# Splitting the row-bound step of the activations' scale, and reordering the parts and squares of the last blocks

## Chip, cores and metric

The program runs on one core of a Trainium2 chip. The metric is the device time of one execution in microseconds. All rows below come from one profiled execution.

## What is computed

One layer of a hybrid encoder, in float32, for 512 tokens of 1024 channels. The two attention-like branches come first; the change touches only the squared-ReLU MLP behind them:

```python
h = rms_norm(x, norm_ffn[l])                                   # (512, 1024)
x = x + jnp.square(jax.nn.relu(h @ w_up[l])) @ w_down[l]       # w_up 1024x4096, w_down 4096x1024
```

## The kernel before

TensorE multiplies float16 pairs: each operand is scaled by a power of two and split into a high and a low half ("part"), and one product is three matmuls (`three`, lines 139 to 142). A part is made by `split` (lines 109 to 116): ScalarE writes the high half (line 114), VectorE the low half (line 115), so VectorE waits for ScalarE each time.

The MLP is 16 blocks in the order of the list `order`: "u" blocks (`up`) are 96 matmuls of 512 columns and write relu and square (ScalarE, lines 1085 and 1088) into an activation tile `a`; "d" blocks (`down`) take a finished pair of "u" blocks. The six "d" blocks 4, 6, 8, 10, 12 and 13 use seven products (a Strassen step), 168 matmuls of 256 columns; blocks 14 and 15 take four products, with 512 columns. While TensorE does block n, ScalarE and VectorE make the parts of the block behind it.

Each scale needs a bound over all 128 partitions, made by class `Scale`. For weights: ScalarE squares four chunks as they land (`top`, line 866, tile `squares`), VectorE sums the row sums (`gather`, line 779, tile `top`), TensorE spreads the sum over the partitions (`spread`, line 792, tile `scale`), and VectorE makes the scale (lines 802 to 807). For activations (`rows[q]`, four of them) `gather(True)` does three things in a row: the row maximum on VectorE (line 779), a transpose of it on TensorE (line 784, tile `tops`), and a maximum along that row on VectorE (line 786, tile `one`); `spread` follows some steps later (line 792, then lines 796 to 799). `tops` and `scale` share one PSUM buffer (tag "o").

The order is written by hand: `at(n, t, f)` puts step f behind tick t of block n (16 ticks of six matmuls in a block of four products, 14 ticks of twelve in one of seven). `pin` keeps the marked instructions of an engine in that order; a scheduler places the rest, so a step can stand some matmuls from its tick. Each engine then works its instructions off in order, and a waiting one holds up all behind it.

`left_plan` and `last_left` place the parts of the activations (tiles `spare`, `left`, and `a` for the last two blocks); `planned` places load, squares, gather, spread and parts (tile `ring`) of the weights of block m. All loads of weights are issued by SP's queue.

Of the kernel before, what the change touches and what calls it, by code (L numbers as in the profile page):

```python
# [9 lines left out]
F32 = mybir.dt.float32  # L10
F32R = mybir.dt.float32r
BF16 = mybir.dt.bfloat16
# [4 lines left out]
ALU = mybir.AluOpType  # L17
AX = mybir.AxisListType

P = 128  # L20
# [17 lines left out]
def hybrid_layer(ctx: ExitStack, tc: tile.TileContext, x, norm_mix, w_in, a_q_norm, a_k_norm,  # L38
# [25 lines left out]
    def first(ins):  # L64

        return pin(ins) if strict[0] else ins
# [697 lines left out]
    class Scale:  # L764
# [10 lines left out]
        def gather(self, closely=False):  # L775

            self.top = sm.tile([P, 1], F32 if closely else BF16, tag="top", name="top")
            with nc.allow_low_precision(reason="a bound"):
                pin(nc.vector.tensor_reduce(self.top, self.m[:, 0:self.n + 1], axis=AX.X,
                                            op=ALU.max if self.prior is None else ALU.add))  # L780
            self.rows = ones16
            if closely:
                ps = pm.tile([P, 512], F32, tag="o", name="tops")
                pin(nc.tensor.transpose(ps[0:1, 0:P], self.top, ident))
                self.top = sm.tile([1, 1], BF16, tag="one", name="one")
                first(nc.vector.tensor_reduce(self.top, ps[0:1, 0:P], axis=AX.X, op=ALU.max))
                self.rows = ones16[0:1, :]

        def spread(self):

# [192 lines left out]
    def at(n, t, f):  # L983

        plan.setdefault((n, t), []).append(f)
# [13 lines left out]
    def several(n, steps, fs):  # L999
        for t, f in zip(steps, fs, strict=True):  # L1000
            at(n, t, f)

    def planned(m):

        b = blocks[m]

        def make():
            several(m - 1, steps, b.pieces())

        tops = [lambda c=c: b.top(c) for c in range(4)]  # L1010
        if m > 1:
            several(m - 2, range(4), [lambda c=c: b.load(c) for c in range(4)])
            if not b.seven and blocks[m - 1].seven and m < 14:
                several(m - 2, (9, 13), tops[:2])
                several(m - 1, (0, 2), tops[2:])
                at(m - 1, 4, lambda: b.scale.gather())
            else:
                several(m - 2, (4, 6, 8, 10), tops)
                at(m - 2, 12, lambda: b.scale.gather())
        if b.seven:  # L1020
            spread, steps = 2, (0, 1, 3, 4, 5, 6, 7, 8, 9, 10, 11)
        else:
            spread, steps = {1: (2, (8, 9, 10, 11)), 3: (2, (3, 4, 5, 6))}.get(
                m, (8, (9, 10, 11, 12)))
        at(m - 1, spread, lambda: b.scale.spread())
        at(m - 1, -1, make)
# [88 lines left out]
    def left_plan(q, n, steps):  # L1115

        def f():
            for (m, t), piece in zip(steps, left_pieces(q), strict=True):
                at(m, t, piece)
        at(n, -1, f)  # L1120

    for q, n, g, w in ((0, 2, 2, 6), (1, 4, 2, 8), (2, 8, 2, 8), (3, 12, 2, 8)):
        at(n, g, lambda q=q: rows[q].gather(True))
        at(n, w, lambda q=q: rows[q].spread())
    left_plan(0, 2, [(2, 3), (2, 4)] + [(2, t) for t in range(7, 16)])
    for q, n in ((1, 5), (2, 9)):
        left_plan(q, n, [(n, 12), (n, 13)] + [(n + 1, t) for t in (2, 4, 6, 7, 8)]
                  + [(n + 2, t) for t in (12, 13, 14, 15)])
# [1 line left out]
    def last_left():  # L1130
        t = act.tile([P, 4, 1024], F32, tag="uh", name="a16")
        lefts[3] = [pair(t[:, c], KC) for c in range(4)]
        several(13, (5, 6, 7, 8), [
            lambda c=c: split(*lefts[3][c], raws[3][:, KC * c:KC * c + KC], scale=rows[3].by)
            for c in range(4)])

# [95 lines left out]
```

## Time and profile before

| | us |
|---|---|
| median of 3 executions | 724.7 |
| lowest, highest | 721.67, 725.2 |
| the profiled execution | 722.87 |
| its span, first to last instruction | 721.2 |
| TensorE busy in the span | 701.8 |
| VectorE busy | 449.6 |
| ScalarE busy | 400.7 |
| mean granted TensorE clock, as a share of 2.4 GHz | 0.995 |

Busy time is counted over the whole span. TensorE's matmuls overlap (each row's duration is its latency, while the next one starts after a fraction of it), so a hold of TensorE is read from the start of one row to the start of the next. The MLP takes the last half of the span, from about 365 us on.

### The profile page before, as it was taken

Reading aid. Unit: us, or ns where it says so; the run is one execution under the profiler, and the core shown is the slowest. Engines: PE = TensorE matmul, PEld = TensorE weight load, DVE = VectorE, ACT = ScalarE, POOL = GpSimd, SP = SyncE. Lnnn points to the kernel's source line nnn. Section 1 sums busy time; section 2 is a strip of 40 time slices with the busy share of each in tenths; the row PEclk is TensorE's granted clock in tenths of the full one; section 3 lists DMA queues with packets and bytes.
Section 4 is the critical chain, followed back from the end, with each engine's and each line's share of the span. In section 5 each row is a group of like instructions: output and inputs, shape, how many; then the busy total and the mean of one; then the engine's idle time right before and its main releaser. Section 6 shows DMA issues by size and latency. Waiting matters only on the chain.

```text
span 721.2 us, 9785 instructions
## 1 busy us (share of the span) xinstructions
PE 701.8 (97%) x3910; PEld 509.8 (71%) x3910; DVE 449.6 (62%) x679; ACT 400.7 (56%) x617; POOL 58.5 (8%) x73
## 2 busy tenths in 40 slices
PE   7999999999999999999999999989998999989898
PEld 5777778888877888888888644475755758478444
DVE  5548375845656553627664247767787778788961
ACT  6444444444454852334175677795969487775520
POOL 4300124100000000304010000000000000000000
PEclk9999999999999999999999999999999999999999
DMA  6703412222222523464133033033333222333011
GB/s 238 237 33 89 117 59 64 83 60 87 62 85 60 175 77 100 146 212 139 58 122 113 1 117 117 1 117 117 118 118 117 85 83 75 110 117 102 31 45 58
DMA packets 37903, 71.08 MB, mean 99 GB/s; under 512 B 3745, under 2 KB 5089, under 8 KB 37858
## 3 DMA queue, kind: packets, MB, share of 16 engines
q1 hardware_dynamic: 37858, 70.47, 30.0%
q8 instruction: 30, 0.49, 0.3%
q14 instruction: 15, 0.12, 0.1%
HBM read 68.36 MB, written 2.10 MB: 98 GB/s over the span
## 4 chain that ended last, share of the span: by engine, by line
PE 67%; DVE 15%; ACT 11%; issue 4%; DMA 1%; POOL 1%; SPq 0%; DVEq 0%; ACTq 0%; POOLq 0%
PE g L140 20%; PE g L142 19%; PE g L141 19%; DVE ring L115 5%; ACT ring L114 4%; DVE left L115 3%; ACT squares L866 3%; PE poa L663 2%; DVE raw L884 1%; ACT relu L1085 1%; DVE spare L884 1%; ACT a L1088 1%; ACT left L114 1%; PE pt L75 1%; DVE x L1169 1%
## 5 line engine op out<-in xcount | busy, mean ns | idle before, releaser
L114 ACT ACTIVATE ring<-raw,bound 128x1024 f16<-128x1024 f32 x70 | 77.0, 1137 | 59.6 <-DVE bound L807 28.1
L115 DVE SCALAR_TENSOR_TENSOR ring<-raw,bound,ring 128x1024 f16<-128x1024 f32 x70 | 87.8, 1280 | 30.6 <-ACT ring L114 30.6
L140 PE MATMUL g<-h,ring 128*128 128x512 f16 (+1 forms) x288 | 102.3, 355 | 0.0
L142 PE MATMUL g<-h,ring 128*128 128x512 f16 (+1 forms) x288 | 102.3, 355 | 0.0
L141 PE MATMUL g<-h,ring 128*128 128x512 f16 (+1 forms) x288 | 102.3, 355 | 0.0
L112 DVE TENSOR_TENSOR wl<-wst,wh 128x1024 fp32r<-128x1024 f32 x48 | 59.6, 1244 | 62.5 <-ACT wh L111 62.3
L111 ACT CAST wh<-wst 128x1024 fp32r<-128x1024 f32 x48 | 50.3, 1049 | 69.4 <-PE g L141 46.5
L142 PE MATMUL g<-ring,left 128*128 128x256 f16 x288 | 79.3, 275 | 0.0
L140 PE MATMUL g<-ring,left 128*128 128x256 f16 x288 | 79.3, 275 | 0.0
L141 PE MATMUL g<-ring,left 128*128 128x256 f16 x288 | 79.2, 275 | 0.0
L866 ACT ACTIVATE squares<-raw,bound 128x1024 bf16<-128x1024 f32 x60 | 68.1, 1135 | 4.2 <-DMA raw<-in_w_down_dram 4.2
L140 PE MATMUL g<-uh,wh 128*128 128x512 f32 x160 | 64.9, 406 | 0.0
L142 PE MATMUL g<-uh,wl 128*128 128x512 f32 x160 | 62.6, 391 | 0.0
L141 PE MATMUL g<-ul,wh 128*128 128x512 f32 x160 | 62.5, 391 | 0.0
L140 PE MATMUL g<-wh,uh 128*128 128x512 f32 x128 | 52.9, 413 | 0.3 <-DVE qt L458 0.3
L141 PE MATMUL g<-wl,uh 128*128 128x512 f32 x128 | 50.1, 391 | 0.0
L142 PE MATMUL g<-wh,ul 128*128 128x512 f32 x128 | 50.1, 392 | 0.0
L142 PEld LDWEIGHTS <-ring 128*128 128x128 f16 x288 | 28.2, 98 | 27.5 <-DVE ring L115 0.5
L140 PEld LDWEIGHTS <-ring 128*128 128x128 f16 x288 | 28.2, 98 | 26.8 <-issue 0.8
L141 PEld LDWEIGHTS <-ring 128*128 128x128 f16 x288 | 28.2, 98 | 25.5
L142 PEld LDWEIGHTS g<-uh,wl 128*128 128x128 f32 x160 | 30.0, 188 | 6.6
L141 PEld LDWEIGHTS g<-ul,wh 128*128 128x128 f32 x160 | 30.2, 189 | 5.7 <-issue 0.2
(276 smaller groups left out, 1395.1 us busy)
## 6 DMA issues: line engine op xcount, KB each, us to landing
wst<-in_w_in_dram SPq DMA_DIRECT2D x41, 512.0 KB, 3.7
raw<-in_w_up_dram SPq DMA_DIRECT2D x32, 512.0 KB, 4.7
raw<-in_w_down_dram SPq DMA_DIRECT2D x32, 512.0 KB, 5.0
wst<-in_w_branch_dram SPq DMA_DIRECT2D x8, 512.0 KB, 3.9
wst<-in_w_out_dram SPq DMA_DIRECT2D x8, 512.0 KB, 4.5
xs<-in_x_dram SPq DMA_DIRECT2D x4, 512.0 KB, 6.1
x<-in_x_dram SPq DMA_DIRECT2D x4, 512.0 KB, 7.7
out_dram<-x SPq DMA_DIRECT2D x7, 256.0 KB, 2.0
```

The costliest lines, as they stand in the source:

```text
L75: ins = nc.tensor.transpose(out[:, i, :], block, ident)
L111: first(nc.scalar.copy(hi, src))
L112: first((engine or nc.vector).tensor_tensor(lo, src, value(hi), op=ALU.subtract))
L114: first(nc.scalar.activation(hi, src, AF.Identity, scale=scale))
L115: first(nc.vector.scalar_tensor_tensor(lo, src, scale, value(hi), op0=ALU.mult, op1=ALU.subtract))
L140: nc.tensor.matmul(ps, ah, bh, start=start, stop=False)
L141: nc.tensor.matmul(ps, ah, bl, start=False, stop=False)
L142: nc.tensor.matmul(ps, al, bh, start=False, stop=stop)
L663: nc.tensor.matmul(po[:, h, :], pT[0][:, k, :], av[:, k, h * P:(h + 1) * P], start=(k == 0), stop=(k == t))
L866: pin(nc.scalar.activation(junk, self.chunk(c), AF.Square, scale=self.scale.prior.by, accum_out=m))
L884: return lambda: pin(nc.vector.tensor_tensor(d, a, b, op=sub))
L1085: pin(nc.scalar.activation(r, ps, AF.Relu, scale=inv))
```

## The change

The step of the activations' bound is cut in three. `gather()` keeps only the row maximum; a new method `closest` holds the transpose and the second maximum; `spread` is as before. The ticks move from 2 (row maximum, transpose, second maximum together) and 6 or 8 (spread) to 4, then 7 or 8, then 10 or 12. The parts of activation q = 0 begin later to match. For the last blocks, the spread of block 14's weights moves from tick 8 to tick 2 of block 13 and its parts from ticks 9 to 12 to ticks 3 to 6; the parts of the last activation move from ticks 5 to 8 to ticks 7 to 10; the squares of block 15's weights move from ticks 4 to 10 to ticks 9 to 13, and their gather from tick 12 of block 13 to tick 2 of block 14.

```diff
@@ class Scale
             self.rows = ones16
-            if closely:
-                ps = pm.tile([P, 512], F32, tag="o", name="tops")
-                pin(nc.tensor.transpose(ps[0:1, 0:P], self.top, ident))
-                self.top = sm.tile([1, 1], BF16, tag="one", name="one")
-                first(nc.vector.tensor_reduce(self.top, ps[0:1, 0:P], axis=AX.X, op=ALU.max))
-                self.rows = ones16[0:1, :]
+
+        def closest(self):
+
+            ps = pm.tile([P, 512], F32, tag="o", name="tops")
+            pin(nc.tensor.transpose(ps[0:1, 0:P], self.top, ident))
+            self.top = sm.tile([1, 1], BF16, tag="one", name="one")
+            first(nc.vector.tensor_reduce(self.top, ps[0:1, 0:P], axis=AX.X, op=ALU.max))
+            self.rows = ones16[0:1, :]
@@ planned
-                several(m - 2, (4, 6, 8, 10), tops)
-                at(m - 2, 12, lambda: b.scale.gather())
+                several(m - 2, (4, 6, 8, 10) if m < 15 else (9, 11, 12, 13), tops)
+                at(*((m - 2, 12) if m < 15 else (14, 2)), lambda: b.scale.gather())
...
-            spread, steps = {1: (2, (8, 9, 10, 11)), 3: (2, (3, 4, 5, 6))}.get(
+            spread, steps = {1: (2, (8, 9, 10, 11)), 3: (2, (3, 4, 5, 6)), 14: (2, (3, 4, 5, 6))}.get(
@@
-    for q, n, g, w in ((0, 2, 2, 6), (1, 4, 2, 8), (2, 8, 2, 8), (3, 12, 2, 8)):
+    for q, n, g, c, w in ((0, 2, 4, 7, 10), (1, 4, 4, 8, 12), (2, 8, 4, 8, 12), (3, 12, 4, 8, 12)):
         at(n, g, lambda q=q: rows[q].gather(True))
+        at(n, c, lambda q=q: rows[q].closest())
         at(n, w, lambda q=q: rows[q].spread())
-    left_plan(0, 2, [(2, 3), (2, 4)] + [(2, t) for t in range(7, 16)])
+    left_plan(0, 2, [(2, 3), (2, 8)] + [(2, t) for t in range(11, 16)] + [(3, t) for t in range(4)])
@@ last_left
-        several(13, (5, 6, 7, 8), [
+        several(13, (7, 8, 9, 10), [
```

Where the steps stand in the built programs is counted in matmuls from the start of a block. The transpose `tops` stands behind matmul 21 of block 2, 46 of block 4, 42 of block 8 and 74 of block 12 before, and behind 48, 111, 111 and 108 now. The spread of the activation's scale stood behind 42, 111, 111 and 108 of the same blocks, and stands behind 66, 156, 156 and 166. The spread of block 14's scale moves from behind 108 of block 13 to behind 63. SP's and POOL's queues are in the same order in both programs.

**VectorE in block 8.** In the rows, `left` are parts of activation q = 1, `sums` and `x` are the results of the products of the block, `top` twice the row maximum of activation q = 2 and then the sum for block 9's or 10's weights, and `scale` the spread of block 9's scale. Before:

```order
L115 SCALAR_TENSOR_TENSOR left_3506<-a,bound,left_3506 128x1024 x2
L1169 SCALAR_TENSOR_TENSOR sums<-g,inv,sums 128x512
L779 TENSOR_REDUCE top<-bound 128x1
L786 TENSOR_REDUCE one<-tops 1x1
L1169 SCALAR_TENSOR_TENSOR x_2709<-g,inv,x_2709 128x2x256
L779 TENSOR_REDUCE top<-bound 128x1
L1169 SCALAR_TENSOR_TENSOR x_2709<-g,inv,x_2709 128x2x256 x2
L1169 SCALAR_TENSOR_TENSOR sums<-g,inv,sums 128x512
L802 TENSOR_SCALAR bound<-scale 128x1
```

and now:

```order
L115 SCALAR_TENSOR_TENSOR left_3506<-a,bound,left_3506 128x1024 x2
L1172 SCALAR_TENSOR_TENSOR sums<-g,inv,sums 128x512
L1172 SCALAR_TENSOR_TENSOR x_2709<-g,inv,x_2709 128x2x256
L779 TENSOR_REDUCE top<-bound 128x1 x2
L1172 SCALAR_TENSOR_TENSOR x_2709<-g,inv,x_2709 128x2x256 x2
L1172 SCALAR_TENSOR_TENSOR sums<-g,inv,sums 128x512
L804 TENSOR_SCALAR bound<-scale 128x1
L807 SCALAR_TENSOR_TENSOR bound<-bound 128x1
L809 RECIPROCAL bound<-bound 128x1
L1083 TENSOR_TENSOR inv<-bound,gs 128x1
L886 TENSOR_TENSOR spare<-raw 128x1024
L788 TENSOR_REDUCE one<-tops 1x1
```

The second maximum `one` moved from right behind the row maximum to behind block 9's scale and one subtraction.

**VectorE in blocks 12 and 13.** `ring` are low halves of block 13's weights, each of which waits for its high half on ScalarE; the row L115 `ring_2747<-spare` makes the part of the fourth product. Before:

```order
L807 RECIPROCAL bound<-bound 128x1
L779 TENSOR_REDUCE top<-bound 128x1
L1141 TENSOR_TENSOR inv<-bound 128x1
L1158 TENSOR_SCALAR minus<-inv 128x1
L786 TENSOR_REDUCE one<-tops 1x1
L1169 SCALAR_TENSOR_TENSOR x_2709<-g,inv,x_2709 128x2x256
L115 SCALAR_TENSOR_TENSOR ring<-raw,bound,ring 128x1024 x2
```

and now:

```order
L809 RECIPROCAL bound<-bound 128x1
L1172 SCALAR_TENSOR_TENSOR x_2709<-g,inv,x_2709 128x2x256
L1144 TENSOR_TENSOR inv<-bound 128x1
L1161 TENSOR_SCALAR minus<-inv 128x1
L115 SCALAR_TENSOR_TENSOR ring<-raw,bound,ring 128x1024
L779 TENSOR_REDUCE top<-bound 128x1
L115 SCALAR_TENSOR_TENSOR ring<-raw,bound,ring 128x1024
L1172 SCALAR_TENSOR_TENSOR x_2709<-g,inv,x_2709 128x2x256 x2
L115 SCALAR_TENSOR_TENSOR ring<-spare,bound,ring 128x1024
L886 TENSOR_TENSOR spare<-raw,spare 128x1024
L1172 SCALAR_TENSOR_TENSOR sums<-g,inv,sums 128x512
L115 SCALAR_TENSOR_TENSOR ring_2747<-spare,bound,ring_2747 128x1024
L788 TENSOR_REDUCE one<-tops 1x1
```

The row maximum of the last activation now stands behind the low half of block 13's first part, and its second maximum behind that of the fourth.

**ScalarE in block 13.** `ring_2748` are the last two parts of block 13, `ring` parts of block 14 (and, at the end, of block 15), `a_5613` parts of the last activation, `squares` those of block 15's weights. Before:

```order
L114 ACTIVATE ring_2748<-raw,bound 128x1024 x2
L866 ACTIVATE squares,bound<-raw,bound 128x1024
L114 ACTIVATE a_5613<-a,bound 128x1024
L866 ACTIVATE squares,bound<-raw,bound 128x1024
L114 ACTIVATE a_5613<-a,bound 128x1024 x2
L866 ACTIVATE squares,bound<-raw,bound 128x1024
L114 ACTIVATE a_5613<-a,bound 128x1024
L114 ACTIVATE ring<-raw,bound 128x1024
L866 ACTIVATE squares,bound<-raw,bound 128x1024
L114 ACTIVATE ring<-raw,bound 128x1024 x7
```

and now:

```order
L114 ACTIVATE ring_2748<-raw,bound 128x1024 x2
L114 ACTIVATE ring<-raw,bound 128x1024 x4
L114 ACTIVATE a_5613<-a,bound 128x1024 x2
L868 ACTIVATE squares,bound<-raw,bound 128x1024
L114 ACTIVATE a_5613<-a,bound 128x1024 x2
L868 ACTIVATE squares,bound<-raw,bound 128x1024 x3
L114 ACTIVATE ring<-raw,bound 128x1024 x4
```

All four parts of block 14 now stand ahead of the last activation's, and three of the four squares behind both.

## Rows read from the trace of the kernel before

**Rows 1.** The page, part 1: busy us, share of the span, instructions.

```profile
PE 701.8 (97%) x3910; PEld 509.8 (71%) x3910; DVE 449.6 (62%) x679; ACT 400.7 (56%) x617; POOL 58.5 (8%) x73
```

**Rows 2.** Waits of TensorE, the longest: us in total, times, longest us.

```profile
PE tops L784 <- DVE top L779: 7.3, 3, 3.0
```

**Rows 3.** Timeline, block 4: start us, us, engine, line, form [idle before <-releaser].

```profile
472.69 0.27 PE L140 MATMUL g<-ring,left 128*128 128x256 f16 x1
...
474.92 0.17 DVE L779 TENSOR_REDUCE top<-bound 128x1 f32<-128x9 f32 x1 [2.19 <-ACT a L1088]
475.13 0.27 PE L784 MATMUL tops<-ident,top 128*1 128x128 f32 x1 [2.18 <-DVE top L779]
...
475.44 0.28 DVE L786 TENSOR_REDUCE one<-tops 1x1 bf16<-1x128 f32 x1 [0.36 <-PE tops L784]
```

**Rows 4.** Timeline, block 8, TensorE at the same place.

```profile
553.12 0.27 PE L142 MATMUL g<-ring,left 128*128 128x256 f16 x1
...
555.55 0.27 PE L784 MATMUL tops<-ident,top 128*1 128x128 f32 x1 [2.16 <-DVE top L779]
```

**Rows 5.** Busy by windows: PE, PEld, DVE, ACT, POOL, granted clock, DMA, GB/s.

```profile
475.00:480.00 5.00, 4.87 (x45) 4.37 (x46) 2.62 (x6) 4.98 (x9) 0.00 (x0) 1.00 0.81 307
555.00:560.00 5.00, 4.45 (x26) 3.35 (x27) 1.60 (x5) 5.00 (x9) 0.00 (x0) 0.66 0.04 12
640.00:645.00 5.00, 2.57 (x24) 2.31 (x25) 4.66 (x11) 2.83 (x6) 0.00 (x0) 1.00 0.10 38
675.00:680.00 5.00, 5.00 (x17) 1.92 (x16) 5.00 (x7) 2.02 (x2) 0.00 (x0) 0.66 0.00 0
```

**Rows 6.** Timeline, spread of block 9's scale, its first matmul, its fourth part.

```profile
564.77 0.16 DVE L802 TENSOR_SCALAR bound<-scale 128x1 int32<-128x1 int32 x1 [0.59 <-PE scale L792]
...
571.32 0.38 PE L140 MATMUL g<-h,ring 128*128 128x512 f16 x1
...
572.84 1.27 DVE L115 SCALAR_TENSOR_TENSOR ring<-raw,bound,ring 128x1024 f16<-128x1024 f32 x1
```

**Rows 7.** Timeline, block 12, TensorE and ScalarE at the transpose.

```profile
639.17 0.27 PE L141 MATMUL g<-ring,left 128*128 128x256 f16 x1
...
642.36 1.15 ACT L114 ACTIVATE ring<-raw,bound 128x1024 f16<-128x1024 f32 x1 [2.17 <-DVE bound L807]
642.43 0.27 PE L784 MATMUL tops<-ident,top 128*1 128x128 f32 x1 [2.99 <-DVE top L779]
...
642.54 0.27 PE L142 MATMUL g<-ring,left 128*128 128x256 f16 x1
```

**Rows 8.** Timeline, VectorE, parts of block 13 and gather of block 14.

```profile
651.98 1.28 DVE L115 SCALAR_TENSOR_TENSOR ring<-spare,bound,ring 128x1024 f16<-128x1024 f32 x1 [0.55 <-ACT ring L114]
653.18 0.15 DVE L796 TENSOR_SCALAR bound<-scale 128x1 int32<-128x1 int32 x1
...
653.63 1.21 DVE L884 TENSOR_TENSOR raw<-spare,raw 128x1024 f32<-128x1024 f32 x1
654.76 0.75 DVE L1169 SCALAR_TENSOR_TENSOR x<-g,minus,x 128x512 f32<-128x512 f32 x1
656.06 1.28 DVE L115 SCALAR_TENSOR_TENSOR ring<-raw,bound,ring 128x1024 f16<-128x1024 f32 x1 [0.56 <-ACT ring L114]
...
661.29 0.15 DVE L779 TENSOR_REDUCE top<-bound 128x1 bf16<-128x5 f32 x1
```

**Rows 9.** Timeline, TensorE: block 13's first and last, block 14's first two, block 15's first.

```profile
653.01 0.27 PE L140 MATMUL g<-ring,spare 128*128 128x256 f16 x1
...
671.27 0.27 PE L142 MATMUL g<-ring,left 128*128 128x256 f16 x1
672.82 0.38 PE L140 MATMUL g<-ring,a 128*128 128x512 f16 x1 [1.27 <-ACT ring L114]
674.61 0.38 PE L141 MATMUL g<-ring,a 128*128 128x512 f16 x1 [1.42 <-DVE ring L115]
...
696.83 0.38 PE L140 MATMUL g<-ring,a 128*128 128x512 f16 x1
```

## The prediction, made before the changed kernel had run

> **What bounds the kernel.** I read the page's first part, then TensorE's waits, then the timeline around each wait, then the granted clock around them. TensorE is busy in 97% of the span [rows 1], so the time is its work plus what holds it up, and a gain must come from a hold. In the MLP, the waits that the trace names on TensorE are few, and the largest by far is that of the transpose `tops` for the row maximum `top`: 7.3 us in three waits [rows 2]. TensorE works in order, so all matmuls behind the transpose are held too.
>
> The three holds, from the slot that the transpose would have had. One matmul of 256 columns takes (671.27 - 653.01) / 167 = 0.109 us from start to start [rows 9]. Block 4: 475.13 - (472.69 + 0.11) = 2.33 us [rows 3]. Block 8: 555.55 - 553.23 = 2.32 [rows 4]. Block 12: 642.43 - 639.28 = 3.15 [rows 7]. In blocks 4 and 8 it is ScalarE that is late with the last square of the row sums; VectorE waited 2.19 us for it in block 4 [rows 3]. A fourth hold is block 14's begin: the first matmul comes 672.82 - 671.27 - 0.11 = 1.44 us late, and the second, which wants a low half from VectorE, 674.61 - 672.82 - 0.22 = 1.57 us more (0.22 for twice the columns) [rows 9].
>
> Then the clock. Behind block 8's hold and behind block 14's begin the granted clock of a 5 us window is 0.66 [rows 5], so (1 - 0.66) x 2 x 5 = 3.4 us stood at the lower level, 1.2 GHz, which gives back half: 1.7 us lost each time. Behind the holds of blocks 4 and 12 it stayed at 2.4 GHz, 1.00 [rows 5]. So two holds of four were followed by such a fall.
>
> **The change, block by block.** Nothing is removed: each transpose, maximum and spread is still issued, four of each, and a transpose that waits for nothing keeps the slot it had. No DMA moves and SP's and POOL's order is the same, so the cost lies in what each moved step finds on VectorE and ScalarE.
>
> Blocks 4 and 8. The transpose moves from behind matmul 46 or 42 to behind 111, some 7 us later. The row maximum was ready at 475.1 in block 4; the new slot, with the hold gone, is at 472.80 + 65 x 0.109 = 479.9. In block 8 it is 553.23 + 69 x 0.109 = 560.8, against 555.5 before. One more product's result (`x`) now stands ahead of the maximum on VectorE, of 0.75 us [rows 8], far inside the 5 us. Both holds go: 2.33 + 2.32, and the fall behind block 8's with them, 1.7. The second maximum moves behind block 9's scale and a subtraction, some 2 us, and its spread has 45 matmuls (4.9 us) to wait; nothing shows there. The transpose shares its PSUM buffer with the spread three matmuls ahead of it, as the activation's own spread did before, so that small wait only changes its name.
>
> What could be late next are the parts of blocks 5 and 9, since TensorE comes earlier by the hold and VectorE must not be the one that stayed. VectorE was waiting for TensorE when block 9's scale was spread, 0.59 us of idle [rows 6]; so its work behind that moves along. The fourth part was done 572.84 + 1.2 - 564.77 = 9.3 us behind the spread, and block 9 wants it 571.32 + 18 x 0.22 - 564.77 = 10.5 us behind; the second maximum (0.28 [rows 3]) now lies in between. Margin 0.9 us: no new hold taken, bounds 0 and 1 us for each of the two blocks.
>
> Block 2: its hold is not among the three waits; I take 0, though its parts now reach into block 3, where ScalarE's and VectorE's idle time takes them.
>
> Block 12. Here the order speaks against the change. The row maximum now stands behind the low half of block 13's first part, which waits for ScalarE's high half. That starts at 642.36 and takes 1.15 [rows 7]; the low half then holds VectorE 1.2 (651.98 to 653.18 [rows 8]), and from the maximum to the transpose go 0.21 [rows 3]: 642.36 + 1.15 + 1.2 + 0.21 = 644.92. (All times of blocks 12 to 15 are on the clock of the kernel before, as if nothing had been saved earlier; VectorE and ScalarE are in step with TensorE at block 9, so the whole moves along.) TensorE arrives at the new slot, behind 108 matmuls instead of 74, at 639.28 + 34 x 0.109 = 642.99. It waits 1.93 us instead of 3.15.
>
> Then a new wait. The spread stands behind matmul 166 now, at 645.03 + 58 x 0.109 = 651.37, and wants the second maximum, which stands behind the fourth part's low half. That ends VectorE's turn at 653.18 [rows 8]; plus 0.28 [rows 3] and some 0.05 it is 653.51: 2.14 us of wait where before none was taken. Block 13 begins at 653.83 instead of 653.01 [rows 9]: 0.8 us later.
>
> Block 13. VectorE saves the three short rows of the scale, 653.63 - 653.18 = 0.45, and pays 0.2 for the second maximum; so all that follows comes 0.25 earlier, block 14's gather at 661.04 instead of 661.29 [rows 8]. The spread of block 14's scale stands behind matmul 63, at 653.83 + 63 x 0.109 = 660.7, and shares its buffer with the activation's spread, which VectorE reads only behind that gather: some 661.33. A wait of 0.6, with the slot 0.7. Bounds 0 and 1.5, since it is a difference of two chains.
>
> Block 14. Its scale is ready at some 662.8: behind the gather come the activation's scale (0.45), a result (0.75) and its own three rows. The four high halves follow on ScalarE, to some 667, and the low ones on VectorE from 664.0: four parts at 1.2 and three results at 0.75, to 671.05. The last activation's low halves are then done at 672.25, 673.45, 675.4 and 676.6, with one result between the second and the third (durations [rows 8]). TensorE ends block 13 at 653.83 + 168 x 0.109 + 0.7 = 672.9 and wants them, each with the third matmul of its group, at 673.3, 674.7, 676.0 and 677.3. The margin is 0.6 us at the least: the hold of 1.44 + 1.57 is gone, and the fall behind it, 1.7. The squares of block 15 come later, but the spread that needs them stands behind matmul 54 of block 14, at 684.7, and ScalarE, with eight more steps of at most 1.15 us [rows 7] behind 667, is done by 676; nothing waits.
>
> From block 12 on: block 15 starts at 672.9 + (696.83 - 672.82 - 1.57 - 1.7) = 693.6 instead of 696.83: 3.2 less.
>
> **Sum.** 2.3 + 2.3 + 1.7 + 3.2 = 9.5 us off the profiled execution's 722.87: 713.4. The two waits in block 12 are some 2 us long, and two holds of four of such length were followed by a fall; so I count one fall, 1.7: **715.1**, put at 715. With none it is 713.4, with two 716.8. The median of the executions, 724.7, lies 1.8 above the profiled one, and they spread over 3.5, about two falls; so I sum against the profiled one and let the falls make the range.
>
> What the trace shows is that equal holds differ: 2.32 us was followed by a fall, 2.33 and 3.15 were not [rows 3 to 5, 7]. The Trainium skill (page "TensorE: Matmul & The Clock Gate", section "What's actually happening") says that the monitor behind the clock runs freely and does not start with the kernel, so that the same kernel meets it in another phase at each run. By that rule each of the two waits can be followed by a fall in one execution and not in the next, and the sum would move between 713.4 and 716.8 from run to run; one profile cannot show it.
>
> **Rivals.** (a) VectorE and ScalarE are less late in block 12 than read, as they are freed of work ahead: then the waits of 1.9, 2.1 and 0.6 shrink and no fall follows, 709 to 712. Against: their order up to there is unchanged, and they are busy in 4.66 and 2.83 of 5 us in that window, where TensorE has only 2.57 [rows 5]. 0.1. (b) The last activation's parts are late, since they now stand behind all four of block 14's: the margin of 0.6 is used up, block 14 waits 1 to 3 us again and a fall may follow, 717 to 720. For it: TensorE's hold there was on VectorE's low half already [rows 9]. 0.15. (c) The maximum still comes too late in blocks 4 and 8, so that the change does not do what it says: 715 + 4 to 6, 719 to 721. Against: 5 us of room in both. 0.03. (d) Slower: the waits of block 12 leave the clock at 1.2 GHz for long, in blocks 13 to 15. It decides from about 13 us lost, 26 us at half clock, eight times the 3.4 us that either fall lasted: 728 and more. Against: both falls ended by themselves while TensorE worked on [rows 5]. 0.02.
>
> **Chances and range.** The forecast has 0.7. The range 711.0 to 718.5 holds it whole with its falls and margins, and half of (a) and of (b); some 0.18 is left out. Faster by over 0.5% than the median (under 721.1; about what a measurement of this kernel can tell from no change) are the forecast, (a), (b) and most of (c): 0.95. Within it 0.03, slower 0.02.
>
> **What would show it.** TensorE's waits: no transpose wait in blocks 4 and 8, one of 1.9 us in block 12, a new one of `scale` for `one` of 2.1 us near block 12's end, 0.6 us of `scale` in block 13, none at block 14's first matmuls. The granted clock: no low window behind block 4, 8 or at block 14. It is wrong if block 12's waits sum to far from 4 us, if parts of blocks 5, 9 or 14 are waited for, or if low windows stand elsewhere.

## The result, and the profile after the change

The changed kernel takes 714.1 us (713.4 to 715.2), the kernel before 724.8 beside it: ratio 0.986, interval 0.983 to 0.989. Run twice more it gave 715.0 (0.989, 0.987 to 0.991) and 714.1 (0.988, 0.986 to 0.990). One execution of the first repeat took 1833 us; it and its profile are left out. The prediction was 715.0, range 711.0 to 718.5. The profiled execution has 714.4 us and a span of 712.7.

The page, part 1, against [rows 1]: TensorE is busy for 2.3 us less, in a span 8.5 us shorter.

```profile
PE 699.5 (98%) x3910; PEld 509.2 (71%) x3910; DVE 449.1 (63%) x679; ACT 400.1 (56%) x617; POOL 58.5 (8%) x73
```

TensorE's waits in the MLP (us in total, times, longest), against [rows 2]. (Line numbers are those of the changed kernel, two or three higher from the new method on; `tops` is now L786.) Of 7.3 us for the row maximum 1.8 are left, in block 12; the wait for `one` is new.

```profile
PE scale L794 <- DVE one L788: 2.0, 1, 2.0
PE tops L786 <- DVE top L779: 1.8, 1, 1.8
...
PE tops L786 <- DVE bound L804: 0.5, 1, 0.5
```

Block 12 in the timeline (start, us, engine, line, form [idle before <-releaser]), against [rows 7]. From matmul to transpose 638.73 - 636.68 - 0.11 = 1.94 us are lost, from matmul to spread 647.29 - 645.06 - 0.11 = 2.12; both end right behind VectorE's row.

```profile
636.68 0.27 PE L142 MATMUL g<-ring,left 128*128 128x256 f16 x1
638.52 0.15 DVE L779 TENSOR_REDUCE top<-bound 128x1 f32<-128x9 f32 x1
638.73 0.27 PE L786 MATMUL tops<-ident,top 128*1 128x128 f32 x1 [1.78 <-DVE top L779]
...
645.06 0.27 PE L140 MATMUL g<-ring,left 128*128 128x256 f16 x1
...
646.96 0.27 DVE L788 TENSOR_REDUCE one<-tops 1x1 bf16<-1x128 f32 x1
...
647.29 0.16 PE L794 MATMUL scale<-one,ones 1*128 1x1 bf16 x1 [1.96 <-DVE one L788]
```

Block 14's begin, against [rows 9]: the two gaps of the kernel before, 1.44 and 1.57 us, are gone.

```profile
667.53 0.27 PE L142 MATMUL g<-ring,left 128*128 128x256 f16 x1
667.64 0.38 PE L140 MATMUL g<-ring,a 128*128 128x512 f16 x1
667.86 0.38 PE L141 MATMUL g<-ring,a 128*128 128x512 f16 x1
```

Windows (busy us of PE, PEld, DVE, ACT, POOL, granted clock, DMA share, GB/s), against [rows 5]. Behind block 8's transpose and at block 14 the clock now stays at 2.4 GHz. One fall is there, behind block 12's second wait: (0.26 + 0.09) x 2 x 5 = 3.5 us at 1.2 GHz.

```profile
555.00:560.00 5.00, 5.00 (x49) 4.30 (x46) 3.63 (x9) 4.19 (x7) 0.00 (x0) 1.00 0.00 0
...
645.00:650.00 5.00, 3.04 (x18) 1.98 (x16) 3.89 (x6) 3.46 (x5) 0.00 (x0) 0.74 0.02 3
650.00:655.00 5.00, 5.00 (x44) 4.30 (x43) 3.77 (x5) 2.76 (x4) 0.00 (x0) 0.91 0.00 0
...
670.00:675.00 5.00, 5.00 (x25) 2.25 (x24) 4.96 (x8) 0.57 (x2) 0.00 (x0) 1.00 0.00 0
```

By stretches, between first matmuls: the MLP up to block 4 gains 467.77 - 467.14 = 0.63 us; block 4 to 12 takes 624.98 - 467.14 = 157.84 us against 631.17 - 467.77 = 163.40; block 12 to 14 takes 667.64 - 624.98 = 42.66 against 41.65; block 14 itself 688.39 - 667.64 = 20.75 against 24.01 [rows 9]. So 0.63 + 5.56 - 1.01 + 3.26 = 8.44 us, the difference of the two profiled executions (722.87 - 714.44). Of it nothing comes from blocks 12 and 13, which took longer. First matmuls of blocks 4 and 12 before, then of blocks 4, 12 and 15 now:

```profile
467.77 0.27 PE L140 MATMUL g<-ring,spare 128*128 128x256 f16 x1
631.17 0.27 PE L140 MATMUL g<-ring,spare 128*128 128x256 f16 x1
```

```profile
467.14 0.27 PE L140 MATMUL g<-ring,spare 128*128 128x256 f16 x1
624.98 0.27 PE L140 MATMUL g<-ring,spare 128*128 128x256 f16 x1
...
688.39 0.38 PE L140 MATMUL g<-ring,a 128*128 128x512 f16 x1
```

### The profile page after: what moved, and what is told of

It is laid out like the page before. It is cut to its first block, busy times and chain, and to the rows that moved or that the text cites. A ratio compares the mean times of both kernels' runs of the same rounds, so it can differ in the third digit from the quotient of the medians.

```text
span 712.7 us, 9784 instructions
## 1 busy us (share of the span) xinstructions
PE 699.5 (98%) x3910; PEld 509.2 (71%) x3910; DVE 449.1 (63%) x679; ACT 400.1 (56%) x617; POOL 58.5 (8%) x73
## 4 chain that ended last, share of the span: by engine, by line
PE 78%; DVE 9%; ACT 8%; issue 3%; POOL 1%; DMA 0%; SPq 0%; DVEq 0%; ACTq 0%; POOLq 0%
PE g L140 23%; PE g L142 23%; PE g L141 23%; ACT ring L114 3%; DVE ring L115 3%; ACT squares L868 2%; PE poa L663 2%; DVE left L115 2%; ACT relu L1087 1%; PE pt L75 1%; DVE spare L886 1%; DVE raw L886 1%; ACT left L114 1%; PE ps L591 1%; DVE x L1172 1%
## 5 line engine op out<-in xcount | busy, mean ns | idle before, releaser
L115 DVE SCALAR_TENSOR_TENSOR ring<-raw,bound,ring 128x1024 f16<-128x1024 f32 x70 | 87.8, 1280 | 31.6 <-ACT ring L114 31.6
```

The source lines that it names most:

```text
L115: first(nc.vector.scalar_tensor_tensor(lo, src, scale, value(hi), op0=ALU.mult, op1=ALU.subtract))
```

## The experiments

Each kernel is the changed kernel (`after`) with the edit shown. Below, a "fall" is a stretch of some 3.4 us at 1.2 GHz. Each execution has a mean granted clock beside its time: 1.000 is none, 0.997 or 0.998 one, 0.995 two, 0.992 or 0.993 three falls (3.4 us at half the clock lower the mean by 3.4 / 2 / 713 = 0.0024). In the tables of the code, `(q, n, g, c, w)` are the activation, its block and the steps of maximum, transpose and spread.

**The two halves apart.** First the row maximum of blocks 2, 4 and 8 alone:

```
-    for q, n, g, c, w in ((0, 2, 4, 7, 10), (1, 4, 4, 8, 12), (2, 8, 4, 8, 12), (3, 12, 4, 8, 12)):
+    for q, n, g, c, w in ((0, 2, 4, 7, 10), (1, 4, 4, 8, 12), (2, 8, 4, 8, 12), (3, 12, 2, 2, 8)):
...
-                several(m - 2, (4, 6, 8, 10) if m < 15 else (9, 11, 12, 13), tops)
-                at(*((m - 2, 12) if m < 15 else (14, 2)), lambda: b.scale.gather())
+                several(m - 2, (4, 6, 8, 10), tops)
+                at(m - 2, 12, lambda: b.scale.gather())
...
-            spread, steps = {1: (2, (8, 9, 10, 11)), 3: (2, (3, 4, 5, 6)), 14: (2, (3, 4, 5, 6))}.get(
+            spread, steps = {1: (2, (8, 9, 10, 11)), 3: (2, (3, 4, 5, 6))}.get(
...
-        several(13, (7, 8, 9, 10), [
+        several(13, (5, 6, 7, 8), [
```

> Only the three steps of the row maximum in blocks 2, 4 and 8 are moved apart; block 12 and the last blocks are as in the kernel before. Theory (holds of TensorE add up): gone are block 4's hold less the 0.65 us that the changed kernel still waits there (1.7), block 8's hold (2.3), the clock's fall behind it (1.7) and 0.6 in blocks 2 and 3: 6.3 off, 718.5 us. Block 12's wait for the row maximum stays near 3.0 us and block 14's begin is still held by some 3 us. Rival (VectorE and ScalarE, which did not come earlier, take it back): the time saved in blocks 4 and 8 returns as longer waits in blocks 12 to 14, 721 to 724 us.

Measured 715.8 us against 723.2 (ratio 0.992, 0.989 to 0.995, with one execution of 725.8 us in it), which is 2.7 under what was expected. The difference is one of falls: ten of its twelve executions had one, the median execution of the kernel before has two (0.995). Put like to like, one fall each, the median is 715.7 against 720.15: 4.4 us, where the three terms (1.7, 2.3 and 0.6) were taken at 4.6. The rival is out, by the times alone: the profiled execution ran at a granted clock of 0.95 throughout (last section), so no row of it stands here.

Then the last blocks alone:

```
-    for q, n, g, c, w in ((0, 2, 4, 7, 10), (1, 4, 4, 8, 12), (2, 8, 4, 8, 12), (3, 12, 4, 8, 12)):
+    for q, n, g, c, w in ((0, 2, 2, 2, 6), (1, 4, 2, 2, 8), (2, 8, 2, 2, 8), (3, 12, 2, 2, 8)):
...
-    left_plan(0, 2, [(2, 3), (2, 8)] + [(2, t) for t in range(11, 16)] + [(3, t) for t in range(4)])
+    left_plan(0, 2, [(2, 3), (2, 4)] + [(2, t) for t in range(7, 16)])
```

> Only the last blocks are changed (block 14's scale spread early in block 13, its parts ahead of block 15's squares, the last activation's parts two steps later); the row maximum is handled as in the kernel before in all four places. Theory (holds add up): block 14's hold (3.0 us) and the clock's fall behind it (1.7) are gone, and some 0.7 us of wait of block 13's scale come: 4.0 off, 720.7 us, with three waits of the transpose, 7.3 us in all, unchanged. Rival (the last activation's parts are now late instead): 1 to 3 us of hold at block 14 are left, 722 to 724 us.

Measured 720.4 us (ratio 0.996, 0.995 to 0.998). TensorE's waits:

```profile
PE tops L786 <- DVE top L779: 7.3, 3, 3.0
...
PE scale L794 <- DVE top L779: 1.5, 2, 1.3
```

The three transposes wait as before, no wait of block 14 is left, and the longest wait of a scale, in block 13, is 661.61 - 660.01 - 0.11 = 1.49 from matmul to matmul, not 0.7 (the 0.2 beside it was there before, in block 3). With one fall each it is 718.7 against 720.15, with two 720.6 against 722.6. The changed kernel is 5.5 us under the kernel before with one fall (714.7) and 6.3 with two (716.3, a single execution), the halves are 4.4 + 1.4 and 4.4 + 2.0: they add up within 0.4 us. The split in block 12 is in neither half; it comes next.

**What sets blocks 12 and 13.** Block 12 put back alone:

```
-    for q, n, g, c, w in ((0, 2, 4, 7, 10), (1, 4, 4, 8, 12), (2, 8, 4, 8, 12), (3, 12, 4, 8, 12)):
+    for q, n, g, c, w in ((0, 2, 4, 7, 10), (1, 4, 4, 8, 12), (2, 8, 4, 8, 12), (3, 12, 2, 2, 8)):
```

> The changed kernel with block 12 alone put back: maximum, transpose and spread of the last activation's scale stand as in the kernel before. Theory (waits on TensorE add up, and block 12's two waits cost more than its one did): one wait of some 3.15 us instead of 1.94 and 2.12, so 0.9 us less than the changed kernel, and 1.7 less still where no fall of the clock follows: 711.5 to 713.2 us against 714.1. Rival (VectorE sets when block 14 can begin, whatever TensorE waits for in block 12): the 0.9 us return as a wait of block 13's scale or at block 14's first matmuls, 713.6 to 714.6 us.

Measured 714.0 us (0.989, 0.986 to 0.991): the rival. From block 12 to 14 it takes 41.69 us without a fall, the changed kernel without a fall 41.61 (table below). So the split in block 12 is worth nothing. The one wait of 3.0 is back, the two are gone, and block 13's scale is waited for longer:

```profile
PE tops L786 <- DVE top L779: 3.0, 1, 3.0
PE scale L794 <- DVE top L779: 1.3, 1, 1.3
```

One edit more on the changed kernel, the maximum one step earlier:

```
-    for q, n, g, c, w in ((0, 2, 4, 7, 10), (1, 4, 4, 8, 12), (2, 8, 4, 8, 12), (3, 12, 4, 8, 12)):
+    for q, n, g, c, w in ((0, 2, 4, 7, 10), (1, 4, 4, 8, 12), (2, 8, 4, 8, 12), (3, 12, 3, 8, 12)):
```

> The changed kernel with one edit: the row maximum of block 12 is taken one step earlier, so that it stands on VectorE ahead of the low half of block 13's first part. The first wait of block 12 (1.94 us) shrinks to some 0.2. Theory (VectorE's own chain sets when the second maximum is there, at 646.96 us in the changed kernel): the second wait, of the spread, grows by as much, from 2.1 to some 3.9 us, and the time stays, 713.6 to 714.6 us. Rival (the two waits are independent): the second stays 2.1 us, and 1.7 us are saved, 712.4 us.

Measured 714.9 us (0.990, 0.988 to 0.992), 0.3 above the range of the theory. All six executions had a fall; the five with one took 714.4 to 715.3, the changed kernel with one 714.4 to 715.2. TensorE at the spread:

```profile
643.12 0.27 PE L140 MATMUL g<-ring,left 128*128 128x256 f16 x1
647.21 0.16 PE L794 MATMUL scale<-one,ones 1*128 1x1 bf16 x1 [3.81 <-DVE one L788]
```

The first wait is gone, and the second has grown from 2.12 to 647.21 - 643.12 - 0.11 = 3.98. The spread comes at 647.21, where it came at 647.29: VectorE has the second maximum when it has it, and a wait taken away ahead of that is handed on in full.

**The parts of block 14 and the squares of block 15.**

```
-                several(m - 2, (4, 6, 8, 10) if m < 15 else (9, 11, 12, 13), tops)
-                at(*((m - 2, 12) if m < 15 else (14, 2)), lambda: b.scale.gather())
+                several(m - 2, (4, 6, 8, 10), tops)
+                at(m - 2, 12, lambda: b.scale.gather())
```

> The changed kernel with the squares of block 15 put back to where they were, in block 13 between the parts of block 14; the early spread of block 14's scale and all else stay. If the early spread carries the gain (ScalarE had 4.9 us of idle in block 13): the last activation's last part is some 1 us later on VectorE, with about 1 us of room; 0 to 1 us of wait at block 14, 714.0 to 715.0. Rival (the squares held block 14 up in the kernel before): its hold of some 3 us comes back, 716.5 to 718.5.

Measured 715.0 us (0.989, 0.987 to 0.991), and in the one execution without a fall 714.3, against 713.4 to 713.7 of the changed kernel. So the hold of block 14 does not need the squares moved: the early spread of its scale, with the later parts of the last activation, carries the gain (these two were not tried apart). Block 14 itself takes 0.7 us more (21.45 against 20.75): its matmuls lose 0.23 us at the first part and 670.51 - 669.85 - 0.22 = 0.44 us at the third:

```profile
669.85 0.38 PE L141 MATMUL g<-ring,a 128*128 128x512 f16 x1
670.51 0.39 PE L142 MATMUL g<-ring,a 128*128 128x512 f16 x1 [0.28 <-DVE a L115]
```

**Block 4's small wait.** In the changed kernel the transpose in block 4 waits for VectorE's reading of the spread in the PSUM buffer that it takes. VectorE comes to it late: the sum for block 5's scale waited 4.36 us for ScalarE's squares, and two results (`x`, 1.40) stood in between. The first line holds two rows: the sum (five columns), and right behind it the row maximum of the activation (nine columns).

```profile
478.27 0.23 DVE L779 TENSOR_REDUCE top<-bound 128x1 bf16<-128x5 f32 x2 [4.36 <-ACT squares L868]
478.41 1.40 DVE L1172 SCALAR_TENSOR_TENSOR x<-g,inv,x 128x512 f32<-128x512 f32 x2
...
479.73 0.14 DVE L804 TENSOR_SCALAR bound<-scale 128x1 int32<-128x1 int32 x1
...
479.93 0.27 PE L786 MATMUL tops<-ident,top 128*1 128x128 f32 x1 [0.48 <-DVE bound L804]
```

```
-    for q, n, g, c, w in ((0, 2, 4, 7, 10), (1, 4, 4, 8, 12), (2, 8, 4, 8, 12), (3, 12, 4, 8, 12)):
+    for q, n, g, c, w in ((0, 2, 4, 7, 10), (1, 4, 4, 9, 12), (2, 8, 4, 9, 12), (3, 12, 4, 8, 12)):
```

> The changed kernel with one edit: in blocks 4 and 8 the transpose stands one step later, nine matmuls further behind the spread whose PSUM buffer it takes. The wait of 0.5 us (0.65 from matmul to matmul) for that buffer in block 4 is gone. Theory (in blocks 4 to 11 TensorE sets the time): 0.65 us less than the changed kernel, 713.4. Rival (VectorE sets it there already): the same time within 0.2 us, and a wait of as much for a part in block 5 or 6.

Measured 714.2 us (0.988, 0.986 to 0.990), and with equal falls the same as the changed kernel (none: 713.7 to 714.0; one: 714.4 to 714.9). The wait in block 4 is gone, and block 7 waits for a low half instead, 529.15 - 528.24 - 0.22 = 0.69:

```profile
528.24 0.38 PE L141 MATMUL g<-h,ring 128*128 128x512 f16 x1
529.15 0.39 PE L142 MATMUL g<-h,ring 128*128 128x512 f16 x1 [0.53 <-DVE ring L115]
```

Block 4 to block 8 takes 79.25 us, with the wait 79.21. So here too the wait was handed on, to a later block than the rival said.

**The changed kernel again,** beside the three kernels around it, and once more beside the next two:

> The changed kernel itself once more, beside the three kernels below and on the same chip: some 714.0 us. In the timed executions the mean granted clock tells how many falls of 3.4 us there were (1.000 none, 0.998 one, 0.995 two). If a fall costs its full 1.7 us, executions at 0.998 are 1.7 us longer than those at 1.000; if VectorE sets when block 14 can begin, they differ by some 1 us only, since 0.6 us of block 13's wait goes when TensorE is slow there.

> The changed kernel itself, beside the two kernels above on the same chip: 714.0 to 715.0 us, one fall of the clock in most executions (mean granted clock 0.998).

The changed kernel's 15 executions fall into groups: 713.4 to 713.7 us with no fall (5), 714.4 to 715.2 with one (9), 716.3 with two (1). A profile without a fall (of the last group) shows what the first one hid, block 13's scale, at 655.23 - 654.53 - 0.11 = 0.59 us:

```profile
654.53 0.27 PE L142 MATMUL g<-ring,left 128*128 128x256 f16 x1
655.23 0.16 PE L794 MATMUL scale<-top,ones 128*128 128x1 bf16 x1 [0.43 <-DVE bound L798]
```

**Work taken off VectorE.** One subtraction of block 13's parts goes to GpSimd:

```
-            return [minus(t, b12, b11), minus(b12, b22, b12), put(0, b11), put(1, b21),
+            return [minus(t, b12, b11), minus(b12, b22, b12, nc.gpsimd if self.n == 13 else nc.vector), put(0, b11), put(1, b21),
```

> The changed kernel with one edit: of block 13's parts one subtraction that is not wanted soon (1.2 us on VectorE, ahead of the row maximum in block 12) is done by GpSimd instead. Theory (VectorE's chain sets what TensorE waits for from block 12 to block 14): all that follows on VectorE comes 1.2 us earlier, and so does block 14; 1.2 us less than the changed kernel, 712.8. Rival (TensorE, or ScalarE with its high halves, sets it): the waits of block 12 only change places, within 0.3 us of the changed kernel. If GpSimd's subtraction, some 2.4 us by the nearest row, disturbs VectorE, it is slower.

Measured 715.9 us (0.990, 0.988 to 0.992): no gain. The one execution without a fall took 713.4, as the changed kernel's do. Behind block 12's begin the spread for the second maximum does come 0.9 us earlier (21.4 instead of 22.3 us), but the first wait shrinks to 0.5 and the second grows to 3.2. Ten matmuls (1.1 us) of that are the scheduler's: it put this spread behind matmul 156 instead of 166. Two falls come in a row, 6.9 us, from within that wait on; so they do in three of the six executions. VectorE then waits for TensorE, 3.45 us:

```profile
645.00:650.00 5.00, 3.29 (x17) 2.27 (x17) 4.27 (x5) 3.46 (x6) 0.00 (x0) 0.57 0.02 3
650.00:655.00 5.00, 5.00 (x36) 4.00 (x35) 1.55 (x3) 2.17 (x4) 0.00 (x0) 0.74 0.00 0
```

```profile
653.74 0.75 DVE L1172 SCALAR_TENSOR_TENSOR sums<-g,inv,sums 128x512 f32<-128x512 f32 x1 [3.45 <-PE g L142]
```

**Places, relief, and both.** Three kernels separate where a step waits from when VectorE has its result. Places alone:

```
-            spread, steps = {1: (2, (8, 9, 10, 11)), 3: (2, (3, 4, 5, 6)), 14: (2, (3, 4, 5, 6))}.get(
+            spread, steps = {1: (2, (8, 9, 10, 11)), 3: (2, (3, 4, 5, 6)), 14: (4, (4, 5, 6, 7))}.get(
...
-    for q, n, g, c, w in ((0, 2, 4, 7, 10), (1, 4, 4, 8, 12), (2, 8, 4, 8, 12), (3, 12, 4, 8, 12)):
+    for q, n, g, c, w in ((0, 2, 4, 7, 10), (1, 4, 4, 8, 12), (2, 8, 4, 8, 12), (3, 12, 3, 8, 0)):
...
-        at(n, w, lambda q=q: rows[q].spread())
+        at(n + (q == 3), w, lambda q=q: rows[q].spread())
```

> The places of the run before (row maximum one step earlier, its spread in block 13, block 14's spread two steps later) without anything taken off VectorE. Theory (VectorE sets it): the second maximum is there at 647.2 us as in the changed kernel, TensorE waits 2.5 us for it, now in block 13, and 1 to 2 us for block 14's scale; block 14 begins at most 1.3 us earlier than in the changed kernel, 713.0 to 714.3 us. Rival (the place of a step on TensorE decides): the waits of 1.9 and 2.1 us go, 710.5 to 711.5 us.

Measured 715.4 us (0.990, 0.987 to 0.994). The wait for `one` is there, in block 13, 648.38 - 645.82 - 0.11 = 2.45 us, so the rival is out; but the time is above the theory's 714.3:

```profile
645.82 0.27 PE L142 MATMUL g<-ring,spare 128*128 128x256 f16 x1
648.38 0.16 PE L794 MATMUL scale<-one,ones 1*128 1x1 bf16 x1 [2.29 <-DVE one L788]
```

Block 12 to 14 is 1.0 us shorter than in the changed kernel, both with a fall. In the profiled execution that 1.0 was lost ahead of the MLP, in a stage that the edit does not touch: ScalarE's second cast of the first weights waits 1.67 us for its load, not 0.53, TensorE's first product begins at 10.45 us, not 9.17, and block 4 at 468.19, not 467.14. ScalarE in the changed kernel, then here:

```profile
7.50 1.05 ACT L299 CAST kh<-wst 128x1024 fp32r<-128x1024 f32 x1 [0.53 <-DMA wst<-in_w_in_dram]
```

```profile
8.87 1.04 ACT L299 CAST kh<-wst 128x1024 fp32r<-128x1024 f32 x1 [1.67 <-DMA wst<-in_w_in_dram]
```

The kernel with block 12 put back lost 0.9 us in the same place (its cast waited 1.74). Why the load is late in some executions is open, and so is whether the other executions of this kernel lost it too.

Relief alone (the subtraction on GpSimd, another subtraction ahead of a low half that waited 0.55 us for ScalarE, and a square of block 14 behind the second part, whose low half had waited 0.81):

```
+            fs[6:8] = fs[7:5:-1] if self.n == 13 else fs[6:8]
...
-                several(m - 2, (4, 6, 8, 10) if m < 15 else (9, 11, 12, 13), tops)
+                several(m - 2, (5, 6, 8, 10) if m == 14 else (4, 6, 8, 10) if m < 15 else (9, 11, 12, 13), tops)
```

> The other half of the kernel that had both: VectorE's chain in block 12 is made 2.3 us shorter (one subtraction on GpSimd, one ahead of a low half, one square later), while maximum, transpose and spreads keep the places of the changed kernel; of the spreads the scheduler itself takes the second maximum's ten matmuls, and block 14's scale 27 matmuls, further forward. Theory (TensorE waits for VectorE at a place, and what stands behind that place on TensorE is still to be done): the three waits are some 0.9, 2.0 and 1.6 us, 132 matmuls of 0.109 us follow the last of them, and block 14 begins 41.4 us behind block 12's begin, against 41.6 in the changed kernel without a fall: 713.2 us without a fall, 714.5 with one. Rival (the relief alone carries the gain): 2.3 us less than the changed kernel, 711 to 711.8.

Measured 712.9 us (0.985, 0.983 to 0.988), no fall in five executions: far from the rival, and 0.4 under the theory (713.2); the waits came out 0.4 to 0.5 shorter than worked out:

```profile
PE scale L794 <- DVE one L788: 1.4, 1, 1.4
...
PE scale L794 <- DVE bound L798: 1.0, 1, 1.0
...
PE tops L786 <- DVE top L779: 0.4, 1, 0.4
```

Both edits together:

> The changed kernel with VectorE's chain in block 12 made shorter and the waiting steps placed later. Shorter: one subtraction of block 13's parts on GpSimd (some 0.9 us), one subtraction ahead of a low half that waits for ScalarE (0.55 of idle), one square of block 14 behind block 13's second part (0.8 of idle); 2.3 us in all. Later: the row maximum of block 12 one step earlier, its spread behind the first product step of block 13, block 14's scale spread two steps later. Theory (VectorE sets when block 14 can begin, and holds this small leave the clock up): the second maximum is there at some 644.9 us on the changed kernel's clock and its spread wants it at 644.8, block 14's scale is waited for 1 us, and block 14 begins 3 to 4.4 us earlier: 710.0 to 711.2 us against 714.4 of the kernel of the next but one run. Rival (TensorE's waits are set elsewhere, by ScalarE or by the falls): 713 to 714.5.

Measured 710.9 us (710.7 to 711.0; ratio 0.983, 0.981 to 0.985), as the theory has it, and better than either kernel. The spread for `one` no longer waits, block 14's scale is waited for 652.35 - 651.12 - 0.11 = 1.12 us, and block 14 begins without a gap:

```profile
645.66 0.27 PE L142 MATMUL g<-ring,spare 128*128 128x256 f16 x1
645.87 0.17 PE L794 MATMUL scale<-one,ones 1*128 1x1 bf16 x1
...
651.12 0.27 PE L142 MATMUL g<-ring,left 128*128 128x256 f16 x1
652.35 0.16 PE L794 MATMUL scale<-top,ones 128*128 128x1 bf16 x1 [0.96 <-DVE bound L798]
...
664.05 0.27 PE L142 MATMUL g<-ring,left 128*128 128x256 f16 x1
664.16 0.38 PE L140 MATMUL g<-ring,a 128*128 128x512 f16 x1
```

Side by side, from block 12's first matmul to block 14's (us, from the timelines), with what TensorE lost at the transpose, at the spread for `one` and at block 14's scale (the three kernels that use GpSimd lose 0.5 more at block 13's scale, early in block 12):

| kernel | lost at the three | falls | block 12 to 14 |
|---|---|---|---|
| changed, first profile | 1.94, 2.12, 0 | 1 | 42.66 |
| changed, third | 1.95, 2.12, 0.59 | 0 | 41.61 |
| block 12 put back | 3.15, 0, 1.49 | 0 | 41.69 |
| maximum earlier | 0, 3.98, 0 | 1 | 42.67 |
| one subtraction off | 0.53, 3.22, 0.36 | 2 | 44.31 |
| places alone | 0, 2.45, 0.52 | 1 | 41.65 |
| relief alone | 0.53, 1.60, 1.12 | 0 | 40.66 |
| both | 0, 0.10, 1.12 | 0 | 38.65 |

In the second and third line the losses sum to 4.66 and 4.64: the places are quite other, the sum is VectorE's. Places alone comes to the same with its fall counted as 1.7 (2.45 + 0.52 + 1.7 = 4.67), and so does one subtraction off with its 0.5 (4.6), its two falls not counted. In the first and fourth line no wait stands behind the fall that could hide it: with 1.7 for it they come to 5.7, and block 14 begins 1.05 us later. Only the two kernels that give VectorE less to do and less to wait for come under it: 3.7 and 1.7 with their 0.5.

Why these two differ by 2.0 us, the built programs show. VectorE lets TensorE spread block 14's scale 651.94 - 625.72 = 26.22 us behind block 12's begin with the relief alone and 652.35 - 625.51 = 26.84 with both, so no earlier with both, and TensorE waits 1.12 us for that in either. But what stands behind that wait on TensorE is still to be done: 132 matmuls with the relief alone, 108 with both, which is 24 x 0.109 = 2.6 us. With the relief alone:

```profile
651.94 0.16 PE L794 MATMUL scale<-top,ones 128*128 128x1 bf16 x1 [0.96 <-DVE bound L798]
```

Not all of this is the edit of the places. Block 14's spread stands behind matmul 63 of block 13 in the changed kernel, 62 with places alone and 60 with both, so the two steps in the code moved it little; with the relief alone the scheduler put it forward to 36. Left at 63 it would not have waited, by an estimate from these rows: TensorE would come to it 27 x 0.109 = 2.9 us later, and the wait was 1.1. So some 1.1 of the 2.0 us are the scheduler's, and 0.9 is left to the other places (the row maximum and the spread for `one`), if block 14's parts keep up; a kernel that keeps the spread at 63 was not run.

## Why the prediction was right

**Blocks 4 and 8.** Both holds went, and the fall behind block 8's with them. From block 4 to 12 that is 163.40 - 157.84 = 5.56 us, where 2.33 + 2.32 + 1.7 = 6.35 were taken. Of the 0.79 between them 0.65 is the term taken as nothing, "that small wait only changes its name", since VectorE reads the spread late; the rest is the fall, which cost 1.6 there (block 8 is 3.90 us shorter, 2.32 of it the hold). The later transpose showed that even this term buys nothing alone. Two readings were wrong without cost. In block 8 it was not ScalarE that was late: its last square was done at 554.8, and VectorE took the maximum at 555.35, right behind a result of its own (`sums`, from 554.69). And the "5 us of room" was not there in block 4: the row maximum stands behind the sum of block 5's weights, not ahead of it as the listing of block 8 is explained, and was taken at 478.4 for a slot at 479.3. It had 0.8 us of room there, 3.6 in block 8. That rival (c) stayed away was in block 4 partly luck.

**Block 2.** Taken as 0; from block 0's first matmul (391.48 now, 391.52 before) to block 4's it is 75.66 us instead of 76.25. So 0.6 us came that the sum left out, about as much as block 4's wait took: that these two cancel is luck.

**Block 12.** Two waits of 1.93 and 2.14 were predicted, 1.94 and 2.12 came; block 13 begins 0.8 us later in a profile without a fall (22.65 instead of 21.84 behind block 12's begin).

**Block 13.** Predicted 0.6; 0.59 without a fall, and nothing with one, because TensorE is then behind VectorE. This the sum did not have: it counted a fall at its full 1.7 us on top of the 0.6. A fall costs the changed kernel 42.66 - 41.61 = 1.05 us from block 12 to 14.

**Block 14.** Hold and fall are gone. The margin of 0.6 us, at the third part, is some 0.8 in the profile without a fall (done at 668.97, wanted at 669.77); with the squares put back this part was waited for 0.44. From block 12 to 15 that profile has 687.46 - 625.11 = 62.35 us against 696.83 - 631.17 = 65.66 [rows 9], 3.3 less, where 3.2 stood in the sum.

**The falls.** The sum gave 713.4 with none, 715.1 with one and 716.8 with two; the executions with none, one and two are at 713.4 to 713.7, 714.4 to 715.2 and 716.3. The prediction drew the spread from a rule of the Trainium skill (page "TensorE: Matmul & The Clock Gate", section "What's actually happening"), that the monitor behind the clock runs freely. The executions are in line with it: the same kernel had no fall in five, one in nine and two in one. No run here shows the monitor itself.

**The rivals.** (a), 709 to 712 by shrinking waits, did not come by itself, and the argument against it held: the waits of block 12 came out as read, 1.94 and 2.12. What (a) describes is what the kernel with both edits makes happen, 710.9. (b) to (d) did not occur.

**What was not seen.** The prediction wrote the waits of block 12 as TensorE's losses that add up. They are one loss, VectorE's, shown at several places, and the two waits could have been traded for one of 3.15 or one of 3.98 without a change in time.

## What to carry to other kernels

Where an engine waits several times in a row for the same other engine, sum the waits: if moving a step leaves the sum as it was, the late engine sets the time, and the gain lies in its own idle time (low halves that wait for a high half, work that can go ahead of such a wait). Then place the waiting steps as late as their readers allow, because all that stands behind a wait still has to run, and look in the built program where a scheduler has put them: here it undid part of one edit. And where executions differ, sort them by the granted clock before comparing kernels, and compare stretch by stretch; falls of the clock and one late load hid here as much as an edit is worth.

## What the runs showed of the hardware

**Falls order most of the times.** Of 46 executions of the kernel before that stood beside the first eleven kernels, seven had a mean clock of 0.998 and took 720.0 to 720.3 us, 21 had 0.995 and took 721.6 to 724.0, 13 had 0.993 and took 723.6 to 725.3, and five had 0.990 or 0.991 and took 724.6 to 725.1. So most of its spread of 5 us goes with the number of falls, but not all: one group is 2.5 us wide, and with block 12 put back the four executions with a fall took 713.8 to 714.0, the two without 714.4. The kernels whose longest wait in blocks 12 and 13 was 1.1 and 1.6 us had no fall in nine executions; with 2.1 us (the changed kernel) ten of fifteen had one or two, with 3.15 (block 12 put back) four of six, with 3.2 (the subtraction on GpSimd) five of six, with 4.0 (the maximum earlier) six of six.

**GpSimd lengthens VectorE's work beside it.** The subtraction, 1.22 us on VectorE, took 3.24 on GpSimd, and VectorE's two low halves, the first of which began beside it, took 3.62 us:

```profile
624.09 3.24 POOL L886 TENSOR_TENSOR raw<-raw 128x1024 f32<-128x1024 f32 x1 [238.69 <-DVE spare L886]
626.00 3.62 DVE L115 SCALAR_TENSOR_TENSOR ring<-raw,bound,ring 128x1024 f16<-128x1024 f32 x2 [0.89 <-ACT ring L114]
```

The other two kernels with this subtraction on GpSimd show the same, 3.24 and 3.61. In the changed kernel without it the two low halves took 2.48:

```profile
625.64 2.48 DVE L115 SCALAR_TENSOR_TENSOR ring<-raw,bound,ring 128x1024 f16<-128x1024 f32 x2 [0.89 <-ACT ring L114]
```

So 1.14 of the 1.2 us taken off came back at once. That the second maximum still came 0.9 earlier is because VectorE waited for ScalarE soon behind them anyway, 0.86 us in the changed kernel. The Trainium skill (page "SBUF — State Buffer", section "Who interferes with whom") says that a VectorE instruction with two SBUF inputs contends with a GpSimd instruction that reads SBUF; these rows are in line with it. Whether the best kernel would be as good without GpSimd was not tried.

**A clock of 0.95 almost all along.** One execution each of two kernels ran at a mean clock of 0.948 and 0.950, at 725.8 and 723.0 us, 10.0 and 7.5 above their medians. In the first of them, the profiled execution with the row maximum moved in blocks 2, 4 and 8, the clock is 1.00 up to 12 us and 0.95 in every window from 14 to 670 us (columns as above):

```profile
655.00:660.00 5.00, 5.00 (x47) 4.42 (x45) 4.22 (x5) 3.91 (x5) 0.00 (x0) 0.95 0.00 0
```

What brings it is open.
